# One plain pair of tiles instead of two at the start of three gated inputs, with the token scale moved between the products that follow

## The chip, the cores and the metric

The kernel runs on one core of one Trainium2 chip. The metric is the device time of one execution in microseconds. Three timed executions of the kernel before took 2118.08, 2118.48 and 2118.67 us, so the median is 2118.48 us. The profile comes from one further execution of the same program.

## The reference

A decoder trunk of two layers over 512 tokens with a model width of 1024, in float32. Each layer is a half-weighted gated network, a token mixer (retention in the first layer, attention with forget gates in the second), a second half-weighted gated network, and a gated input embedding; a root-mean-square norm stands ahead of each. What matters here is the gated network, of which there are four:

```python
def rmsnorm(x, w):
    xf = x.astype(jnp.float32)
    y = xf * lax.rsqrt(jnp.mean(xf * xf, axis=-1, keepdims=True) + EPS)
    return (y * w.astype(jnp.float32)).astype(x.dtype)

def swiglu(x, w_in, w_out):
    g, u = jnp.split(x @ w_in, 2, axis=-1)
    return (jax.nn.silu(g) * u) @ w_out
...
        h = h + 0.5 * swiglu(rmsnorm(h, nw[0]), ffn_w_in[i, 0], ffn_w_out[i, 0])
```

`w_in` is 1024 x 5632, that is 22 blocks of 128 gate columns and 22 blocks of 128 up columns.

## The kernel before

Every product is done with split numbers: a weight or an activation x is held as a high part (x rounded to the fast matmul type) and a low part (x minus the high part), and a product is three matmuls: high by high, high by low, low by high. The activations lie with the model width on the partitions and the 512 tokens along the free axis.

**A gated input** is the product of the normalised activations with one block of gate columns and one block of up columns, both 128 wide. There are 22 of these pairs for each of the four networks, which are called the first to fourth gated input here; in the code `i` is 0 to 3. Two loaded tiles of 128 x 1024 belong to each pair, `q` and `r`, and a pair is computed in one of two ways:

- *plain* (`plain` in `ffn`, matmuls on line 636): for each half of the tokens, eight blocks of the width, two outputs and three matmuls, so 96 matmuls of 128 x 256. Both tiles are split into high and low parts.
- *by seven* (class `Strassen`, matmuls on line 559 in `product`): the 2 x 2 block product with seven products in place of eight, each of 12 matmuls of 128 x 256, so 84 matmuls. `begin` does three of them: the first on `q` itself (`b11`), the second and third on two sums of the weights (`t1` on `s[0]`, `t2` on `s[1]`); it then adds partial results in PSUM (lines 584 to 588) and ends with `W.next_sums`, which lets the next pair's sums be built. `rest` does the other four, and `join` two more additions (lines 606 to 608).

The sums are built in `emit_sums_now`: four additions of weight quarters on the vector engine (line 168), each then split by a cast on the scalar engine (line 88) and a subtraction on the vector engine (line 89). One quarter (`x`, tile `a12`) and the `q` tile of most pairs get their low part in another way (`negated`, lines 134 to 136): two passes on the scalar engine, then a DMA from the GpSimd queue that adds the weights from HBM. Pairs marked `direct` split their `q` with lines 88 and 89. Raw weights come on the SP queue (line 80) into four buffers `wraw`; a later load waits until an earlier tile's readers are done with its buffer.

The **norm's token scale** is a number for each token. It isn't applied to the activations but to the products. `n.columns()` sums the squares over the partitions (eight small matmuls, line 367), and takes the inverse root: line 520 on the vector engine, the square root on the scalar engine (line 509, after a load of its table where another one is in), then lines 514 to 517 on the vector engine. `n.rows()` (line 504) turns the result by four matmuls into a row for each partition, which the scalar engine copies out of PSUM (line 498). `gated` then needs it: line 644 multiplies by it, line 645 takes the sigmoid-weighted unit, line 647 multiplies by the other half.

**Start of a gated input.** The list `PLAIN` says how many pairs begin plainly: `(3, 2, 2, 2)`. In the second to fourth gated input, plain pair 0 runs first; it takes the quarters of the activations block by block as the vector and scalar engines deliver them. Plain pair 1 then has the columns and the permission for the first sums at its step 3 (`summed`) and the rows at its step 10 (`scaled`) of 16. Then pairs 2, 3 and so on go by seven, each begun one pair ahead of its rest.

**Order.** Only the tensor engine's order is that of the program. The order on the vector, scalar and GpSimd engines and the queues is laid down by a scheduler when the program is built, from what can run when by its own costs; on the chip each engine then works through its list in that fixed order. PSUM has eight banks of 128 x 512, taken in rotation.

Of the kernel before, what the change touches and what calls it, by code (L numbers as in the profile page):

```python
# [29 lines left out]
KEPT = 7  # L30
STEP = 1024 + 48
WIDE = 2048 + 128
PLAIN = (3, 2, 2, 2)
CHUNKS = [((0, 6), (6, 14), (14, 22)) for n in PLAIN]
H2 = S // 2
HALVES = (slice(0, H2), slice(H2, S))
# [184 lines left out]
def trunk(ctx, tc, a):  # L221
# [16 lines left out]
    W = Weights(tc, wraw, wpool)  # L238

    def unit(pool):  # L240
        return pool.tile([P, S], F32R, name="unit_" + {id(ua): "a", id(ub): "b", id(uc): "c", id(ud): "d"}[id(pool)])
# [4 lines left out]
    for i in range(4):  # L246
        ins = [Pair(i, a["ffn_w_in"][i, m, 0], a["ffn_w_in"][i, m, 1]) for m in range(NF)]
        chunks = CHUNKS[i]
        outs = [[a["ffn_w_out"][i, m][:, k0 * P : k1 * P] for m in range(KB)] for k0, k1 in chunks]
        for m in [PLAIN[i]] + [k1 + 1 for _, k1 in chunks[:-1]]:  # L250
            ins[m].direct = ins[m + 1].direct = True
# [6 lines left out]
    for kind, hd in ret_order:  # L258
        i = at[kind] + (hd if kind in "qk" else 2 * (hd - 1))
# [10 lines left out]
    def plan_ffn(i):  # L270
        ins, outs = ffn_src[i]
        at = PLAIN[i]
        for pair in ins[:at]:
# [54 lines left out]
    def bank():  # L328
        return psum.tile([P, S], F32, name="bank")

    def temp(dtype=F32):
        return tmp.tile([P, S], dtype, name="tmp")
# [7 lines left out]
    def split(src, hi, lo, scale=None):  # L340

        if scale is None:
            high = nc.scalar.copy(hi, src)
            low = nc.vector.tensor_tensor(out=lo, in0=src, in1=hi.bitcast(F32), op=ALU.subtract)
        else:
            high = nc.scalar.activation(hi, src, AF.Identity, scale=scale)
            low = nc.vector.scalar_tensor_tensor(
                out=lo, in0=src, scalar=scale, in1=hi.bitcast(F32), op0=ALU.mult, op1=ALU.subtract
            )
        return high, low  # L350
# [205 lines left out]
    def product(out, w, c, forms, name, first=False):  # L556

        xs = [form[name] for form in forms]
        add = lambda w, x, start, stop: nc.tensor.matmul(  # L559
            out, w, x, start=start, stop=stop, skip_group_check=True  # L560
        )
        for j, (xh, xl) in enumerate(xs):
            wh = w[:, 0, c + j * P : c + (j + 1) * P]
            add(wh, xh, first and j == 0, False)
            add(wh, xl, False, False)
        for j, (xh, xl) in enumerate(xs):
            add(w[:, 1, c + j * P : c + (j + 1) * P], xh, False, j == 3)

    class Strassen:
# [2 lines left out]
        def __init__(self, n):  # L572
            self.n, self.live = n, {}

        def begin(self, pair):
            c0, c1 = HALVES
            forms = self.n.forms
            W.take(pair)
            g, u = bank(), bank()
            product(g[:, c0], pair.t[0], 0, forms, "b11", True)  # L580
            product(g[:, c1], pair.s[0], 0, forms, "t1")
            product(u[:, c1], pair.s[1], 0, forms, "t2", True)
            cc = temp()
            nc.scalar.copy(cc, g)
            nc.vector.tensor_tensor(out=u[:, c1], in0=u[:, c1], in1=cc[:, c0], op=ALU.add)
            u2 = temp()[:, c0]
            nc.scalar.copy(u2, u[:, c1])
            last = nc.vector.tensor_tensor(out=g[:, c1], in0=g[:, c1], in1=u2, op=ALU.add)
            self.live[id(pair)] = g, u, cc
            W.next_sums(last)  # L590
# [20 lines left out]
    def ffn(i, n, nxt, stack, apool, meanwhile=None):  # L611


        ins, outs = ffn_src[i]
        chunks = CHUNKS[i]
        c0, c1 = HALVES
        act, by7 = {}, Strassen(n)

        def plain(m, between={}):

            ws = [W.take(ins[m].q), W.take(ins[m].r)]
            g, u = bank(), bank()
            order = [(k, t) for k in range(KB) for t in range(2)]
            if i == 2:
                order.sort(key=lambda kt: (kt[0] >= KB - 2, kt[1]))
            elif i:
                order.sort(key=lambda kt: kt[1])
            for at, (k, t) in enumerate(order):
                if at in between:
                    between[at]()  # L630
                e = k % 2
                for o, (w, c) in ((g, (ws[e], 0)), (u, (ws[1 - e], 512))):
                    ks = slice(c + k // 2 * P, c + (k // 2 + 1) * P)
                    xh, xl = n.forms[k // 2][f"b{1 + e}{1 + t}"]
                    for q, (x, y) in enumerate(((w[0], xh), (w[0], xl), (w[1], xh))):
                        nc.tensor.matmul(  # L636
                            o[:, HALVES[t]], x[:, ks], y, start=k == t == q == 0, stop=k == KB - 1 and q == 2,
                            skip_group_check=True,
                        )
            return g, u  # L640

        def gated(m, g, u, change_sign):
            sg = temp()
            nc.vector.tensor_tensor(out=sg, in0=g, in1=n.r, op=ALU.mult)
            nc.scalar.activation(sg, sg, AF.Silu)
            if change_sign:
                nc.vector.scalar_tensor_tensor(out=sg, in0=u, scalar=-1.0, in1=sg, op0=ALU.mult, op1=ALU.mult)
            else:
                nc.vector.tensor_tensor(out=sg, in0=u, in1=sg, op=ALU.mult)
            hi, lo = unit(apool), unit(apool)  # L650
            split(sg, hi, lo)
            act[m] = hi, lo

        def out_blocks(c, ms):
            k0, k1 = chunks[c]
            os, ws = [bank() for _ in ms], [W.take(outs[c][m]) for m in ms]
            for k in range(k0, k1):
                js = slice((k - k0) * P, (k - k0 + 1) * P)
                for o, (wh, wl) in zip(os, ws):
                    mm3(o, wh[:, js], wl[:, js], *act[k], k == k0, k == k1 - 1)  # L660
            for m, o in zip(ms, os):
                if m == KB - 1 and c == len(chunks) - 1 and nxt.early and nxt.extra:
                    nxt.corner(range(KB // 2))
                t1 = temp()
                nc.vector.scalar_tensor_tensor(  # L665
                    out=t1, in0=o, scalar=-0.5, in1=n.r, op0=ALU.mult, op1=ALU.mult
                )
                nc.vector.tensor_tensor(out=h[m], in0=h[m], in1=t1, op=ALU.add)
                if c == len(chunks) - 1:
                    nxt.block(m)  # L670

        done = PLAIN[i]
        if i:
            whole = [plain(0)]
        else:
            W.look = LOOKAHEAD + 2
            W.place(ins[1])
            whole = [plain(0)]
            W.look = LOOKAHEAD
            whole.append(plain(1, {12: n.columns}))  # L680
            W.begin(())

        def scaled():
            n.rows()
            for m, (g, u) in enumerate(whole):
                gated(m, g, u, True)

        def summed():
            n.columns()
            W.begin((n.last,) if n.early else ())  # L690

        last = plain(done - 1, {3: summed, 10: scaled} if i else {10: scaled})
        by7.begin(ins[done])
        gated(done - 1, *last, True)
        begun = done + 1
        for c, (k0, k1) in enumerate(chunks):
            for m in range(done, k1):
                if begun < k1:
                    by7.begin(ins[begun])
                    begun += 1  # L700
                by7.rest(ins[m])
                gated(m, *by7.join(ins[m]), False)
            done = k1
            if begun < NF:
                by7.begin(ins[begun])
                begun += 1
            else:
                stack.close()
                if meanwhile:
                    meanwhile()  # L710
            pair = [(0, 1)] if done == NF else [(0,), (1,)]
            for ms in pair + [(m,) for m in range(2, KB)]:
                out_blocks(c, ms)
# [15 lines left out]
    class OutBoth:  # L729
# [5 lines left out]
        def add(self, i, m, ks_=range(4)):  # L735
            srcs, yhi, ylo = self.parts[i]
            if (i, m // 2) not in self.ws:
                self.ws[i, m // 2] = W.take(srcs[m // 2])
            wh, wl = self.ws[i, m // 2]
            for k in ks_:  # L740
                ks = slice((4 * (m % 2) + k) * P, (4 * (m % 2) + k + 1) * P)
                mm3(self.banks[m], wh[:, ks], wl[:, ks], yhi[k], ylo[k], i == 0 and k == 0, i == 1 and k == 3)
# [857 lines left out]
```

## Time and profile before

| | |
|---|---|
| median of three timed executions | 2118.48 us |
| the profiled execution's own time | 2118.82 us |
| its span from the first to the last instruction | 2117.0 us |
| mean granted clock of the tensor engine | 0.999 |
| tensor engine busy | 2102.4 us, 99% of the span |
| vector engine busy | 1573.0 us, 74% |
| scalar engine busy | 1276.7 us, 60% |
| GpSimd busy | 266.6 us, 13% |
| DMA | 299.46 MB, mean 141 GB/s |

The profiled execution is 0.34 us above the median. Between its own time and its span lie 1.8 us of start and end. In the rows of a timeline the first number is the start in microseconds from the span's start, the second the length of the row, then come engine, line, operation, output and input tiles, shapes and the count of merged instructions; a bracket names how long the engine was idle just before and what released it. Matmuls overlap, so the pace of a run of matmuls is read from start to start, not from their lengths. PE is the tensor engine, DVE the vector engine, ACT the scalar engine, POOL GpSimd.

### The profile page before, as it was taken

The page shows a single profiled execution, that of the slowest core. Times are in us where ns is not written, and L with a number is a line of the kernel's source. Part 1 is how long each engine was busy: PE and PEld are TensorE (multiplying, and loading weights), DVE is VectorE, ACT ScalarE, POOL GpSimd, SP SyncE. Part 2 cuts the span into 40 slices and gives each one's busy share as a digit, 9 for nine tenths or more (in the row PEclk, how much of TensorE's full clock was granted, in tenths as well). Part 3 has the DMA queues.
Part 4 walks back from the last instruction along what each step waited for, and adds up shares of the span by engine and source line. Part 5 has one row for each costly group of instructions (what it writes and reads, how often), then busy time and mean ns, then how long its engine had stood idle before and what let it go on. Part 6 is the DMA issues. An engine that isn't in the chain of part 4 may idle for free.

```text
span 2117.0 us, 36225 instructions
## 1 busy us (share of the span) xinstructions
PE 2102.4 (99%) x14155; PEld 1932.4 (91%) x14155; DVE 1573.0 (74%) x2915; ACT 1276.7 (60%) x2201; POOL 266.6 (13%) x282
## 2 busy tenths in 40 slices
PE   9999999999999999999999999999999999999998
PEld 9999998999998898989989999998888899999988
DVE  9786868677667886868768786776675687867775
ACT  8474556555665664737457465555796774645555
POOL 0010100121200010201001010110334200101100
PEclk9999999999999999999999999999999999999999
DMA  6575654666875354846435475563322335755631
GB/s 194 125 176 134 157 139 131 184 190 181 241 200 159 100 140 112 192 125 163 126 106 152 126 177 142 144 150 107 114 88 72 110 101 127 181 141 143 157 110 41
DMA packets 106285, 299.46 MB, mean 141 GB/s; under 512 B 11120, under 2 KB 14704, under 8 KB 106112
## 3 DMA queue, kind: packets, MB, share of 16 engines
q1 hardware_dynamic: 65088, 212.92, 30.8%
q0 software_dynamic: 36336, 76.82, 20.3%
q10 hardware_dynamic: 4688, 7.39, 1.0%
q8 instruction: 111, 1.82, 0.3%
q14 instruction: 62, 0.51, 0.1%
HBM read 284.47 MB, written 12.62 MB: 140 GB/s over the span
## 4 chain that ended last, share of the span: by engine, by line
PE 88%; DVE 4%; issue 4%; ACT 2%; DMA 1%; POOL 0%; SPq 0%; POOLq 0%; ACTq 0%; DVEq 0%
PE bank L559 41%; PE bank L354 12%; PE bank L353 12%; PE bank L355 12%; PE bank L636 4%; PE bank L544 1%; DMA w<-in_ret_p 1%; PE bank L843 1%; PE bank L844 1%; PE bank L845 1%; PE bank L777 1%; PE bank L778 1%; PE bank L779 1%; PE bank L1229 1%; DVE w L89 1%
## 5 line engine op out<-in xcount | busy, mean ns | idle before, releaser
L88 ACT CAST w<-wraw 128x1024 fp32r<-128x1024 f32 (+1 forms) x208 | 210.4, 1018 | 305.0 <-PE bank L355 210.2
L559 PE MATMUL bank<-unit_a,s 128*128 128x256 f32 x2202 | 322.5, 276 | 0.0
L88 ACT CAST s<-sums 128x512 fp32r<-128x512 f32 x372 | 219.9, 617 | 169.5 <-PE bank L559 82.6
L89 DVE TENSOR_TENSOR s<-sums,s 128x512 fp32r<-128x512 f32 x372 | 246.4, 686 | 101.6 <-ACT s L88 101.0
L559 PEld LDWEIGHTS bank<-unit_a,s 128*128 128x128 f32 x2202 | 284.7, 188 | 0.0
L353 PE MATMUL bank<-unit_d,w 128*128 128x512 f32 x656 | 255.7, 390 | 0.3 <-DVE tmp L1246 0.3
L354 PE MATMUL bank<-unit_d,w 128*128 128x512 f32 x656 | 255.3, 389 | 0.0
L355 PE MATMUL bank<-unit_d,w 128*128 128x512 f32 x656 | 255.3, 389 | 0.0
L89 DVE TENSOR_TENSOR w<-wraw,w 128x1024 fp32r<-128x1024 f32 (+1 forms) x186 | 218.3, 1174 | 44.4 <-ACT w L88 44.0
L559 PE MATMUL bank<-unit_b,s 128*128 128x256 f32 x1040 | 220.4, 276 | 0.0
L355 PE MATMUL bank<-unit_a,w 128*128 128x512 f32 (+1 forms) x536 | 198.3, 370 | 1.2 <-DVE w L89 1.2
L353 PE MATMUL bank<-unit_a,w 128*128 128x512 f32 (+1 forms) x536 | 199.4, 372 | 0.0
L354 PE MATMUL bank<-unit_a,w 128*128 128x512 f32 (+1 forms) x536 | 198.3, 370 | 0.1
L665 DVE SCALAR_TENSOR_TENSOR tmp<-bank,rows 128x512 f32<-128x512 f32 x96 | 66.1, 689 | 145.8 <-PE bank L355 145.8
L559 PEld LDWEIGHTS bank<-unit_b,s 128*128 128x128 f32 x1040 | 165.4, 188 | 0.0
L559 PE MATMUL bank<-unit_b,w 128*128 128x256 f32 x837 | 153.6, 281 | 0.5 <-DMA w<-in_ret_p 0.5
L136 POOL DMA_DIRECT2D a<-in_ffn_w_in x80 | 70.2, 877 | 651.2 <-ACT a L135 469.6
L559 PE MATMUL bank<-unit_a,w 128*128 128x256 f32 x978 | 149.6, 278 | 0.0
L559 PE MATMUL bank<-unit_c,s 128*128 128x256 f32 x682 | 149.2, 276 | 0.0
L353 PEld LDWEIGHTS bank<-unit_d,w 128*128 128x128 f32 x656 | 123.2, 188 | 25.8 <-DVE tmp L1246 0.5
L355 PEld LDWEIGHTS bank<-unit_d,w 128*128 128x128 f32 x656 | 123.1, 188 | 25.7
L354 PEld LDWEIGHTS bank<-unit_d,w 128*128 128x128 f32 x656 | 123.2, 188 | 25.1
(350 smaller groups left out, 4810.2 us busy)
## 6 DMA issues: line engine op xcount, KB each, us to landing
wraw<-in_ffn_w_in SPq DMA_DIRECT2D x174, 512.0 KB, 4.4
wraw<-in_ffn_w_out SPq DMA_DIRECT2D x64, 512.0 KB, 4.3
w<-in_ffn_w_in POOLq DMA_DIRECT2D x57, 512.0 KB, 5.6
a<-in_ffn_w_in POOLq DMA_DIRECT2D x79, 256.0 KB, 6.1
wraw<-in_ret_p SPq DMA_DIRECT2D x28, 512.0 KB, 3.6
wraw<-in_ffn_w_out SPq DMA_DIRECT2D x32, 384.0 KB, 3.6
kept<-tmp POOLq DMA_DIRECT2D x40, 256.0 KB, 4.0
wraw<-in_ret_v SPq DMA_DIRECT2D x16, 512.0 KB, 4.5
```

Of the source, the lines that this page charges most:

```text
L88: self.cast = self.nc.scalar.copy(hi, raw)
L89: low.tensor_tensor(out=lo, in0=raw, in1=hi.bitcast(F32), op=ALU.subtract)
L136: self.nc.gpsimd.dma_start(out=lo, in_=src, accum_op=ALU.add)
L353: nc.tensor.matmul(out, wh, xh, start=first, stop=False)
L354: nc.tensor.matmul(out, wh, xl, start=False, stop=False)
L355: nc.tensor.matmul(out, wl, xh, start=False, stop=last)
L544: nc.tensor.matmul(o[:, half], w[:, ks], x, start=k == t == q == 0, stop=k == KB - 1 and q == 2, skip_group_check=True,)
L559: add = lambda w, x, start, stop: nc.tensor.matmul(out, w, x, start=start, stop=stop, skip_group_check=True)
L636: nc.tensor.matmul(o[:, HALVES[t]], x[:, ks], y, start=k == t == q == 0, stop=k == KB - 1 and q == 2, skip_group_check=True,)
L665: nc.vector.scalar_tensor_tensor(out=t1, in0=o, scalar=-0.5, in1=n.r, op0=ALU.mult, op1=ALU.mult)
L777: nc.tensor.matmul(os[t], xh, wh[:, js], start=k == 0, stop=False)
L778: nc.tensor.matmul(os[t], xh, wl[:, js], start=False, stop=False)
```

## The change

`PLAIN` becomes `(3, 1, 1, 1)`, so pair 1 of the second to fourth gated input goes by seven instead of plainly. The permission for the first sums (`W.begin`) moves into plain pair 0, at its step 3. `begin` gets a function that it calls between its first and its second product: pair 1's `begin` has `n.columns` there, pair 2's `begin` has `scaled` (the rows and the gating of plain pair 0). Pair 1's rest follows without a new `begin` ahead of it, and from pair 2 on the order is as it was. The marks `direct` move with `PLAIN` to pairs 1 and 2 (before, 2 and 3). The first gated input stays as it is.

```diff
-PLAIN = (3, 2, 2, 2)
+PLAIN = (3, 1, 1, 1)
...
-        def begin(self, pair):
+        def begin(self, pair, between=None):
             c0, c1 = HALVES
             forms = self.n.forms
             W.take(pair)
             g, u = bank(), bank()
             product(g[:, c0], pair.t[0], 0, forms, "b11", True)
+            if between:
+                between()
             product(g[:, c1], pair.s[0], 0, forms, "t1")
             product(u[:, c1], pair.s[1], 0, forms, "t2", True)
...
         done = PLAIN[i]
+
+        def summed():
+            W.begin((n.last,) if n.early else ())
+
         if i:
-            whole = [plain(0)]
+            whole = [plain(0, {3: summed})]
...
-        def summed():
-            n.columns()
-            W.begin((n.last,) if n.early else ())
-
-        last = plain(done - 1, {3: summed, 10: scaled} if i else {10: scaled})
-        by7.begin(ins[done])
-        gated(done - 1, *last, True)
-        begun = done + 1
+        if i:
+            by7.begin(ins[done], n.columns)
+            by7.begin(ins[done + 1], scaled)
+            begun = done + 2
+        else:
+            last = plain(done - 1, {10: scaled})
+            by7.begin(ins[done])
+            gated(done - 1, *last, True)
+            begun = done + 1
         for c, (k0, k1) in enumerate(chunks):
             for m in range(done, k1):
-                if begun < k1:
+                if begun < min(k1, m + 2):
                     by7.begin(ins[begun])
                     begun += 1
                 by7.rest(ins[m])
```

The scheduler lays the other engines' lists anew around this. Two places in the fourth gated input show how; the numbers behind `s_` and `w_` tell buffers apart, and line numbers from 576 on are two higher in the changed kernel (584 to 588 read 586 to 590).

On the vector engine, from just ahead of the columns' first step (line 520) to the token scale itself (line 517, output `cols`), before:

```order
L168 TENSOR_TENSOR sums<-wraw 128x512
L520 TENSOR_SCALAR cv<-bank 128x4
L89 TENSOR_TENSOR s_19339<-sums,s_19339 128x512
L168 TENSOR_TENSOR sums<-sums,wraw 128x512
L89 TENSOR_TENSOR s_19363<-sums,s_19363 128x512
L168 TENSOR_TENSOR sums<-sums,wraw 128x512
L514 RECIPROCAL cols<-ct 128x4
L168 TENSOR_TENSOR sums<-wraw 128x512
L515 TENSOR_TENSOR ct<-cols 128x4
L89 TENSOR_TENSOR s_19366<-sums,s_19366 128x512
L516 SCALAR_TENSOR_TENSOR ct<-ct,cv 128x4
L517 SCALAR_TENSOR_TENSOR cols<-ct,cols 128x4
```

and in the changed kernel, where `s_19276` is the second sum of pair 2:

```order
L89 TENSOR_TENSOR s_19276<-sums,s_19276 128x512
L168 TENSOR_TENSOR sums<-wraw 128x512
L520 TENSOR_SCALAR cv<-bank 128x4
L587 TENSOR_TENSOR bank<-bank,tmp 128x256
L89 TENSOR_TENSOR s_19278<-sums,s_19278 128x512
L514 RECIPROCAL cols<-ct 128x4
L515 TENSOR_TENSOR ct<-cols 128x4
L590 TENSOR_TENSOR bank<-bank,tmp 128x256
L516 SCALAR_TENSOR_TENSOR ct<-ct,cv 128x4
L168 TENSOR_TENSOR sums<-wraw 128x512
L517 SCALAR_TENSOR_TENSOR cols<-ct,cols 128x4
```

Line 520 now stands behind all sums of pairs 1 and 2 but one split, and the two additions in PSUM that end pair 1's `begin` stand between line 520 and line 517, with a sum of pair 3's freshly loaded weights.

On the scalar engine at the same place, before:

```order
L88 CAST s_19340<-sums 128x512
L88 CAST s_19339<-sums 128x512
L88 CAST s_19363<-sums 128x512
L509 ACT_TABLE_LOAD
L509 ACTIVATE ct<-cv 128x4
L88 CAST s_19366<-sums 128x512
L498 COPY rows<-bank 128x512
```

and in the changed kernel:

```order
L88 CAST s_19276<-sums 128x512
L586 COPY tmp<-bank 128x512
L134 CAST w_19375<-wraw 128x2x512
L88 CAST s_19278<-sums 128x512
L135 ACTIVATE w_19375<-wraw 128x2x512
L509 ACT_TABLE_LOAD
L509 ACTIVATE ct<-cv 128x4
L589 COPY tmp<-bank 128x256
L88 CAST s_19447<-sums 128x512
L498 COPY rows<-bank 128x512
```

The root (line 509) now stands behind the cast of pair 2's second sum, the copy of pair 1's products (586) and both passes over pair 3's `q` (134 and 135, `w_19375`). The buffer of `s_19276` is that of pair 1's first sum, which pair 1's second product reads. In the second gated input the two lists are much the same (the cast of `s_19278` stands ahead of 134 there), without the table load; in the third the copy of pair 1's products (586) stands three casts earlier, and pair 2's `x` (134) ahead of pair 1's first sum.

## The prediction

> **What bounds the kernel now.** First the page's busy times, then the tensor engine's list of waits, then its timeline at the start of each of the three gated inputs that change. The fourth stands for them here, with the fourth pair's products and some of the second and third.
>
> ```profile
> PE 2102.4 (99%) x14155; PEld 1932.4 (91%) x14155; DVE 1573.0 (74%) x2915; ACT 1276.7 (60%) x2201; POOL 266.6 (13%) x282
> ...
> PE bank L504 <- DVE rn L517: 0.9, 1, 0.9
> ...
> 746.92 2.31 PE L636 MATMUL bank<-unit_b,w 128*128 128x256 f32 x18
> ...
> 1138.61 2.31 PE L636 MATMUL bank<-unit_b,w 128*128 128x256 f32 x18
> ...
> 1719.20 2.31 PE L636 MATMUL bank<-unit_b,w 128*128 128x256 f32 x18
> ...
> 1721.35 0.95 PE L367 MATMUL bank<-ones_r,tmp 128*128 128x2 f32 x8
> 1722.16 0.96 PE L636 MATMUL bank<-unit_c,w 128*128 128x256 f32 x6
> ...
> 1727.28 0.60 PE L504 MATMUL bank<-ident,cols 128*128 128x128 f32 x4
> 1727.63 0.96 PE L636 MATMUL bank<-unit_d,w 128*128 128x256 f32 x6
> ...
> 1732.02 0.64 PE L559 MATMUL bank<-unit_b,w 128*128 128x256 f32 x4
> ...
> 1736.18 0.64 PE L559 MATMUL bank<-unit_b,w 128*128 128x256 f32 x4
> ...
> 1740.34 0.39 PE L559 MATMUL bank<-unit_b,w 128*128 128x256 f32 x2
> ...
> 1745.78 0.64 PE L559 MATMUL bank<-unit_b,w 128*128 128x256 f32 x4
> ```
>
> The tensor engine is the bound: busy 99%, and whatever it no longer does is time saved, as long as nothing makes it wait. Its rows also show the one wait of this kind that exists: the transposes (504) once waited 0.9 us for line 517, elsewhere in the program. In the three starts nothing waits there: the columns (367) end at 1722.16, the rows begin at 1727.28, 5.12 us of plain matmuls lie between.
>
> **What is removed and added on the tensor engine.** Plain pair 1 runs from 1719.20 to 1732.02, 12.82 us. Less the columns (1721.35 to 1722.16, 0.81) and the rows (1727.28 to 1727.63, 0.35), which stay, its 96 matmuls take 11.66. By seven, a `begin` takes 4.16 (1732.02 to 1736.18) and a `rest` 5.44 (1740.34 to 1745.78), together 9.60. Each gated input saves 2.06 us, the three 6.2 us.
>
> **What moves closer together.** The columns now stand behind pair 1's first product, the rows behind pair 2's first. A product on `w` has 12 matmuls at 0.12 (18 take 1721.35 - 1719.20 = 2.15), so 1.44; the other two of a `begin` share 4.16 - 1.44, so 1.36 each. From the end of plain pair 0, at t0, the tensor engine would end the columns at t0 + 2.25, pair 1's second product at t0 + 3.61, its third at t0 + 4.97, and wants the scale (517) at t0 + 6.41. Between columns and rows lie 4.16 us in place of 5.12, and the lists of the two other engines have changed more than that. These rows price them:
>
> ```profile
> 1717.00 0.69 DVE L168 TENSOR_TENSOR sums<-wraw 128x512 f32<-128x512 f32 x1
> ...
> 1718.38 0.69 DVE L89 TENSOR_TENSOR s<-sums,s 128x512 fp32r<-128x512 f32 x1
> ...
> 1722.34 0.16 DVE L520 TENSOR_SCALAR cv<-bank 128x4 f32<-128x4 f32 x1 [0.26 <-PE bank L367]
> ...
> 1722.75 1.28 ACT L509 ACT_TABLE_LOAD   x1
> ...
> 1724.04 0.21 ACT L509 ACTIVATE ct<-cv 128x4 f32<-128x4 f32 x1
> ...
> 1726.45 0.16 DVE L517 SCALAR_TENSOR_TENSOR cols<-ct,cols 128x4 f32<-128x4 f32 x1
> ...
> 1733.33 1.05 ACT L134 CAST w<-wraw 128x1024 fp32r<-128x1024 f32 x1
> 1734.28 1.05 ACT L135 ACTIVATE w<-wraw 128x1024 fp32r<-128x1024 f32 x1
> 1735.24 0.60 ACT L88 CAST s<-sums 128x512 fp32r<-128x512 f32 x1
> 1735.75 0.57 ACT L584 COPY tmp<-bank 128x512 f32<-128x512 f32 x1
> 1736.94 0.37 ACT L587 COPY tmp<-bank 128x256 f32<-128x256 f32 x1 [0.62 <-DVE bank L585]
> ...
> 1737.42 0.42 DVE L588 TENSOR_TENSOR bank<-bank,tmp 128x256 f32<-128x256 f32 x1
> ...
> wraw<-in_ffn_w_in SPq DMA_DIRECT2D x174, 512.0 KB, 4.4
> ```
>
> Before, line 520 ran 0.2 us after the columns and 517 was done at 1726.61, 0.7 us ahead of need. Now the scalar engine's root (509) stands behind the cast of pair 2's second sum, and that cast needs the buffer that pair 1's *second product* reads. So the scale can't begin its way before that product has left the array: t0 + 3.61, and the last matmul's 0.17 us of tail. From there, in the fourth gated input (t0 = 1719.20, product gone at 1722.98): cast 0.60, copy 0.5 (1735.24 and 1735.75 are that far apart) to 1724.1. Pair 3's raw weights are there by about then: their buffer is free when pair 1's third sum has been formed, some 0.5 us after t0, and the load takes 4.4. Passes 134 and 135 over them take 0.95 and 1.05 with a cast of 0.55 between: 1726.7. The table takes 1.28, the root 0.21: 1728.2. Then 0.2 to line 514, the copy and addition that end pair 1's `begin` (0.37 and 0.42), 515, 516 and 517 at 0.16 each and a sum of 0.69 between the last two, 1.85 us with their handovers: **the scale at 1730.1, wanted at 1725.6, a wait of 4.5 us**. Behind the waiting transposes stand all matmuls that follow, so the wait counts in full.
>
> The second gated input (t0 = 746.92) needs no table: product gone at 750.7, cast, copy, cast, 134, 135 and root to 754.6, the scale at 756.4, wanted at 753.3: **3.0 us**. The third needs these rows:
>
> ```profile
> 1136.91 0.68 DVE L168 TENSOR_TENSOR sums<-wraw 128x512 f32<-128x512 f32 x1
> ...
> 1138.46 0.62 ACT L134 CAST a<-wraw 128x512 fp32r<-128x512 f32 x1 [0.20 <-PE bank L636]
> ```
>
> There the cast of pair 1's first sum stands behind pair 2's `x` (134), which waits for plain pair 0 to leave its buffer until 1138.46; so pair 1's third sum is formed only at about 1142.1, pair 3's load lands at 1146.6, and two passes, a cast, table and root bring it to 1150.7, the scale to 1152.5. Wanted at 1138.61 + 6.41 = 1145.0: **7.5 us**. Bounds: with the load already landed, the scalar engine's list alone gives 5.5 in the third; with every load 1 us later 8.5, and 5.5 in the fourth. Together 15.0, between 13 and 17.5.
>
> **What the waits do to the clock.** No wait of several microseconds stands inside the trace of before; its two ends are the nearest rows.
>
> ```profile
> 1.59 4.21 PE L338 MATMUL bank<-tmp,ones_r 128*128 128x512 f32 x9 [1.59 <-DVE tmp L336]
> ...
> 5.60 1.41 PE L636 MATMUL bank<-unit_b,w 128*128 128x256 f32 x6
> ...
> 6.84 0.88 PE L636 MATMUL bank<-unit_d,w 128*128 128x256 f32 x6
> ...
> 2105.30 2.33 PE L1413 MATMUL bank<-unit_a,ones_r 128*128 128x512 f32 x9
> ...
> 2107.46 0.56 PE L1422 MATMUL bank<-ones_r,tmp 128*128 128x2 f32 x4
> ...
> 2110.23 0.59 PE L1443 MATMUL bank<-tmp,ones_r 128*128 128x256 f32 x2
> ...
> 2111.00:2112.00 1.00, 0.00 (x0) 0.00 (x0) 1.00 (x4) 0.23 (x1) 0.69 (x2) 1.00 0.26 92
> 2112.00:2113.00 1.00, 0.00 (x0) 0.00 (x0) 0.51 (x2) 0.00 (x0) 0.72 (x2) 0.64 0.63 216
> ```
>
> In the stretches, the number behind POOL is the granted clock. The last matmul ends at 2110.82; 0.64 over the next-to-following microsecond means full clock until 2112.28 and half from then: 1.5 us after the last matmul, with gaps before it. At the start nine matmuls of 128 x 512 take 4.01 us (1.59 to 5.60) against 2.16 for the same nine at full clock (2105.30 to 2107.46), and the next six lose 0.53 (1.41 against 0.88): a cold start loses 2.4 us. A wait costs between nothing (clock held) and 2.4 more. The waits of 4.5 and 7.5 us are three and five times what sufficed at the end, so I take 2.4 for each, and half, 1.2, for that of 3.0, which a busy stretch precedes: 6.0 in all.
>
> [...]
>
> [...]
>
> **What costs nothing.** Each of the three gets one pair more of sums, additions and, for the second and fourth, two DMAs from the GpSimd queue.
>
> ```profile
> 759.74:773.50 13.76, 13.76 (x122) 13.76 (x121) 10.36 (x18) 11.17 (x18) 2.16 (x2) 1.00 0.49 116
> ```
>
> In a stretch of pairs by seven the vector engine is busy 10.36 of 13.76 us, the scalar engine 11.17, the DMA engines half: matmuls cover it, as they do for the twenty other pairs. Uncovered, eight operations of 0.69 would be 5.5 us for each. Pair 1's first two sums are wanted 2.25 and 3.61 us behind t0; in the fourth gated input the vector engine is done with the quarters at about 1716 and needs four steps of 0.65, so they are there by 1719.2, in time. In the third, pair 1's `q` is now split on the vector engine (1.22) in place of a DMA, in a stretch that has about that much room; at worst 1 us, inside the bounds.
>
> **The sum**, against the profiled execution's 2118.82: less 6.2, plus 15.0 of waits, plus 6.0 of clock is 2133.6, +0.70%. The median of the runs lies 0.34 lower, so **2133.3 us**.
>
> **Rivals.**
>
> 1. *The clock holds.* [...] For it: 0.999 over the whole span, in spite of waits of up to 0.9. Against it: the 1.5 us at the end. 2118.5 - 6.2 + 15.0 = 2127.3 (2125 to 2130 by the bounds).
> 2. *The scale is in time, and the saving stands* (the other side): 2118.5 - 6.2 = 2112.3. It takes the root to be free of the casts ahead of it. For it: before, a like list gave it within 4.45 us of the columns (1722.16 to 1726.61), against 4.16 now. Against it: the engines' lists are fixed, and each holds a wait for pair 1's second product ahead of the root. It would turn from slower to faster where the three waits sum to under 6.2, some 2 us each: in the second gated input about 1 us of the scalar engine's work between that product and the root would have to fall away, in the fourth 2.5, in the third 5.5.
> 3. *Waits about as long as the saving*, 4 to 8 us in all with the clock held: 2116 to 2121, no change that can be told. It needs the load and half the scalar work to overlap in a way the lists don't show.
> 4. *More is late*: the loads that pile up behind the waits and the colder clock make later pairs wait as well, each 2 us more: over 2139. Against it: pair 3's `begin`, the next to want sums, comes over 8 us behind the rows.
>
> **How the numbers follow.** The forecast (2128 to 2139, late scale and halved clock) has 0.50, the clock that holds 0.22, the saving that stands 0.10, waits about equal to it 0.08, more late work 0.10. Differences under 0.2% (4.2 us) I count as no change, about what a measurement of this kernel tells. Faster is then 0.10, same 0.08, slower 0.82. For the range: from the late scale with the clock held and a short chain, some way into rival 3, up to where rival 4 begins: 2120 to 2139, which leaves out 0.10 of rival 2, most of rival 4 and a little of rival 3.
>
> **What would show it.** In the timeline of the changed kernel, three idle stretches of the tensor engine ahead of line 504, released by line 517, of about 3, 7.5 and 4.5 us; line 509 starting behind line 135; 36 matmuls fewer on the tensor engine; and matmuls behind each wait at nearly twice their pace, with a granted clock under 1. If line 504 starts 6.4 us behind plain pair 0 in all three, the reasoning on the lists is wrong; if the waits are there and the clock stays at 1.00, only its term is.

## The result, and the profile after

| | before | changed |
|---|---|---|
| median of four timed executions | 2118.57 us | 2132.57 us (2131.78 to 2136.69) |
| ratio, with its 95% interval | | 1.0071 (1.0059 to 1.0083) |
| span of the profiled execution | 2117.0 us | 2130.0 us |
| mean granted clock | 0.999 | 0.996 |
| matmuls | 14155 | 14119 |

The change makes the kernel 14.0 us slower; the forecast was 2133.3 us, 14.8 slower. The changed kernel's list of waits on the tensor engine (what waits, what it waits for, us in total, times, longest) has a new first line:

```profile
PE bank L504 <- DVE cols L517: 13.6, 3, 7.3
PE bank L338 <- DVE tmp L336: 1.6, 1, 1.6
```

Three waits, one in each changed gated input. These are rows of the changed kernel's timeline on the tensor engine. For the second gated input they show the first product of pair 1's `begin`, the columns, the first product of pair 2's `begin`, the transposes with the idle time ahead of them, and the first matmul of pair 3's `begin`; for the third and fourth only the first, the fourth and the last of these (pair 2's `begin` starts at 1146.60 and 1734.36 there).

```profile
747.00 0.64 PE L559 MATMUL bank<-unit_b,w 128*128 128x256 f32 x4
...
748.43 0.95 PE L367 MATMUL bank<-ones_r,tmp 128*128 128x2 f32 x8
...
752.16 0.65 PE L559 MATMUL bank<-unit_b,w 128*128 128x256 f32 x4
...
756.14 0.65 PE L504 MATMUL bank<-ident,cols 128*128 128x128 f32 x4 [2.38 <-DVE cols L517]
...
766.65 0.64 PE L559 MATMUL bank<-unit_b,w 128*128 128x256 f32 x4
...
1141.44 0.65 PE L559 MATMUL bank<-unit_b,w 128*128 128x256 f32 x4
...
1155.48 1.11 PE L504 MATMUL bank<-ident,cols 128*128 128x128 f32 x4 [7.29 <-DVE cols L517]
...
1166.26 0.64 PE L559 MATMUL bank<-unit_b,w 128*128 128x256 f32 x4
...
1729.21 0.64 PE L559 MATMUL bank<-unit_b,w 128*128 128x256 f32 x4
...
1739.90 1.12 PE L504 MATMUL bank<-ident,cols 128*128 128x128 f32 x4 [3.94 <-DVE cols L517]
...
1750.34 0.64 PE L559 MATMUL bank<-unit_b,w 128*128 128x256 f32 x4
```

From the end of plain pair 0 to pair 3's `begin` the kernel before needs 12.82 + 4.16 = 16.98 us (plain pair 1 and pair 2's `begin`). The changed kernel needs 766.65 - 747.00 = 19.65 us in the second gated input and 1166.26 - 1141.44 = 24.82 in the third. In the fourth it is 1750.34 - 1729.21 = 21.13. That is 2.67, 7.84 and 4.15 us more, 14.7 together; the other 2000 us differ by -1.7 in the two profiled executions (their spans by 13.0), 1.2 of it a wait of line 355 for line 89 late in the kernel before that the changed kernel's list does not show.

The scalar engine of the changed kernel in the fourth gated input shows why the scale is late:

```profile
1733.19 0.62 ACT L88 CAST s<-sums 128x512 fp32r<-128x512 f32 x1 [1.07 <-PE bank L559]
1733.84 0.59 ACT L586 COPY tmp<-bank 128x512 f32<-128x512 f32 x1
1734.32 1.05 ACT L134 CAST w<-wraw 128x1024 fp32r<-128x1024 f32 x1
1735.27 0.62 ACT L88 CAST s<-sums 128x512 fp32r<-128x512 f32 x1
1735.79 1.06 ACT L135 ACTIVATE w<-wraw 128x1024 fp32r<-128x1024 f32 x1
1736.86 1.28 ACT L509 ACT_TABLE_LOAD   x1
1738.15 0.21 ACT L509 ACTIVATE ct<-cv 128x4 f32<-128x4 f32 x1
```

The first cast waits for the tensor engine, that is for pair 1's second product to be done with the buffer; then the copy, the two passes, another cast, the table and the root follow without a gap. On the vector engine of the same stretch the columns' first step was done three microseconds before the root, and what comes after the root takes 1.5 us:

```profile
1735.06 0.15 DVE L520 TENSOR_SCALAR cv<-bank 128x4 f32<-128x4 f32 x1
...
1738.39 0.18 DVE L514 RECIPROCAL cols<-ct 128x4 f32<-128x4 f32 x1 [1.78 <-ACT ct L509]
1738.61 0.16 DVE L515 TENSOR_TENSOR ct<-cols 128x4 f32<-128x4 f32 x1
1738.68 0.43 DVE L590 TENSOR_TENSOR bank<-bank,tmp 128x256 f32<-128x256 f32 x1
1739.02 0.15 DVE L516 SCALAR_TENSOR_TENSOR ct<-ct,cv 128x4 f32<-128x4 f32 x1
1739.09 0.69 DVE L168 TENSOR_TENSOR sums<-wraw 128x512 f32<-128x512 f32 x1
1739.69 0.16 DVE L517 SCALAR_TENSOR_TENSOR cols<-ct,cols 128x4 f32<-128x4 f32 x1
```

The busy times of the changed kernel by stretches hold the second loss. Each stretch is 3.41 us long; the columns are length, busy us (and instructions) of the tensor engine, of its weight load, of the vector, scalar and GpSimd engines, then the granted clock, the DMA engines' share and GB/s:

```profile
753.27:756.69 3.42, 1.04 (x10) 0.82 (x9) 2.69 (x10) 2.16 (x5) 1.07 (x1) 1.00 0.74 250
756.69:760.10 3.41, 3.41 (x18) 3.41 (x18) 2.56 (x6) 1.30 (x4) 0.00 (x0) 0.50 1.10 228
760.10:763.51 3.41, 3.41 (x31) 3.41 (x31) 1.80 (x3) 3.25 (x4) 0.00 (x0) 1.00 0.42 147
...
1152.63:1156.05 3.42, 0.57 (x3) 0.57 (x4) 2.04 (x7) 2.15 (x4) 1.07 (x1) 0.50 1.02 302
1156.05:1159.46 3.41, 3.41 (x18) 3.41 (x17) 2.68 (x6) 2.71 (x5) 0.00 (x0) 0.50 0.65 116
...
1739.73:1743.14 3.41, 3.24 (x15) 3.24 (x16) 3.27 (x7) 2.56 (x4) 0.00 (x0) 0.50 0.88 164
```

Behind each wait the clock is 0.50: 18 matmuls fit where 31 fit a stretch later. The engine counts as busy all the while: its busy time is 2103.2 us, 0.8 more than before, although 36 matmuls are gone. Where this time went is read from the clock column.

### The profile page after: what moved, and what is told of

Its sections match the earlier page's. It is cut to its first block, busy times and chain, and to the rows that moved or that the text cites. A ratio compares the mean times of both kernels' runs of the same rounds, so it can differ in the third digit from the quotient of the medians.

```text
span 2130.0 us, 36208 instructions
## 1 busy us (share of the span) xinstructions
PE 2103.2 (99%) x14119; PEld 1933.3 (91%) x14119; DVE 1586.7 (74%) x2947; ACT 1288.9 (61%) x2226; POOL 270.7 (13%) x286
## 4 chain that ended last, share of the span: by engine, by line
PE 90%; DVE 5%; ACT 3%; issue 1%; DMA 1%; POOL 0%; SPq 0%; POOLq 0%; ACTq 0%; DVEq 0%
PE bank L559 43%; PE bank L354 12%; PE bank L353 12%; PE bank L355 12%; PE bank L638 2%; PE bank L851 1%; PE bank L852 1%; PE bank L850 1%; PE bank L544 1%; DMA wraw<-in_ffn_w_in 1%; PE bank L784 1%; PE bank L786 1%; PE bank L785 1%; PE bank L1236 1%; PE bank L1250 0%
## 5 line engine op out<-in xcount | busy, mean ns | idle before, releaser
L88 ACT CAST s<-sums 128x512 fp32r<-128x512 f32 x384 | 227.5, 618 | 185.6 <-PE bank L559 94.8
L559 PE MATMUL bank<-unit_a,s 128*128 128x256 f32 x2259 | 333.4, 277 | 0.0
L89 DVE TENSOR_TENSOR s<-sums,s 128x512 fp32r<-128x512 f32 x384 | 254.3, 686 | 105.8 <-ACT s L88 104.8
L559 PEld LDWEIGHTS bank<-unit_a,s 128*128 128x128 f32 x2259 | 294.4, 189 | 0.0
L89 DVE TENSOR_TENSOR w<-wraw,w 128x1024 fp32r<-128x1024 f32 (+1 forms) x182 | 213.2, 1172 | 39.2 <-ACT w L88 38.8
L559 PE MATMUL bank<-unit_b,s 128*128 128x256 f32 x1076 | 231.1, 279 | 0.0
L559 PEld LDWEIGHTS bank<-unit_b,s 128*128 128x128 f32 x1076 | 172.7, 190 | 0.1
L559 PE MATMUL bank<-unit_b,w 128*128 128x256 f32 x864 | 158.8, 282 | 0.0
L559 PE MATMUL bank<-unit_c,s 128*128 128x256 f32 x706 | 155.7, 278 | 0.0
L559 PE MATMUL bank<-unit_a,w 128*128 128x256 f32 x1005 | 154.1, 278 | 0.0
```

The source lines that it names most:

```text
L88: self.cast = self.nc.scalar.copy(hi, raw)
L89: low.tensor_tensor(out=lo, in0=raw, in1=hi.bitcast(F32), op=ALU.subtract)
L559: add = lambda w, x, start, stop: nc.tensor.matmul(out, w, x, start=start, stop=stop, skip_group_check=True)
```

## The experiments

Each kernel is timed against the kernel before on the same chip. Beside the filled waits, the rows later, the root first and both edits together the kernel before took 2118.29 us; beside the two halves and the third left as it was, it took 2117.60. "Added" is the time from plain pair 0's end to pair 3's `begin` less the 16.98 us of the kernel before, in the second, third and fourth gated input; the changed kernel adds 2.67, 7.84 and 4.15.

**Is the loss behind the waits one of the clock?** Matmuls of no use fill the waits; the transposes then overwrite their bank.

```diff
     def spread(c, fill=()):
         o = bank()
+        for x in fill:
+            nc.tensor.matmul(o[:, 0:H2], ones_r, x, start=True, stop=True, ...)
...
-            n.rows()
+            n.rows((0, 21, 62, 34)[i])
```

> The changed kernel with matmuls of no use put ahead of the transposes (line 504): 21, 62 and 34 of 128 x 256 at about 0.118 us, that is 2.5, 7.3 and 4.0 us, close to the three gaps of 2.55, 7.44 and 4.10 us in its trace. Nothing else moves. My theory (late scale, and a clock that halves because the tensor engine is idle): the scale comes as late as before, but the clock stays at 1.00, and about 5.0 us come back, 2127.5 us. If the 5 us behind the waits come from something else that the wait brings (late sums, late weights, banks), the time stays at 2132.6. If the clock falls for lack of useful progress on other engines, the same.

Measured: 2128.49 us, ratio 1.0045 (1.0031 to 1.0059). The scale is no earlier, so this kernel waits as long as the changed one, only busily. In its timeline:

```profile
753.53 2.54 PE L505 MATMUL bank<-unit_b,ones_r 128*128 128x256 f32 x21
756.09 0.65 PE L507 MATMUL bank<-ident,cols 128*128 128x128 f32 x4
...
1153.95 0.65 PE L507 MATMUL bank<-ident,cols 128*128 128x128 f32 x4 [0.30 <-DVE cols L520]
```

(its lines from 504 on are three higher.) Its clock stays 1.00 in all three stretches behind the transposes:

```profile
756.00:760.00 4.00, 3.98 (x36) 3.91 (x36) 3.96 (x8) 3.00 (x5) 0.00 (x0) 1.00 1.07 257
1153.00:1160.00 7.00, 6.70 (x58) 6.50 (x57) 5.67 (x12) 5.07 (x8) 0.00 (x0) 1.00 0.72 156
1736.00:1743.00 7.00, 7.00 (x62) 6.85 (x62) 5.58 (x12) 5.22 (x8) 0.00 (x0) 1.00 0.82 193
```

Added: 0.83, 6.08 and 2.38, together 5.4 us less than in the changed kernel. The time is 4.1 us lower by the medians and 5.5 by the two ratios. So some 5 us were lost to the clock, because the engine stood idle, and not to work that came late behind the waits.

**Is it the late scale?** The rows and the gating of plain pair 0 are wanted later, behind the first product of pair 1's `rest`, and nothing else is changed.

```diff
-            by7.begin(ins[done + 1], scaled)
+            by7.begin(ins[done + 1])
...
-                by7.rest(ins[m])
+                by7.rest(ins[m], scaled if i and m == 1 else None)
```

> The changed kernel with the rows and the gating of plain pair 0 moved from between the first two products of pair 2's begin to behind the first product of pair 1's rest, 4.4 us later for the tensor engine; the lists of the vector and scalar engines up to the token scale are row for row those of the changed kernel. Theory (nothing but the late scale costs): the scale is there 9.05, 13.95 and 10.6 us behind plain pair 0 and is wanted at 10.9, so only the third gated input still waits, 3.0 us, with some 1.7 us of clock: 2118.6 - 4.4 + 3.0 + 1.7 = 2118.9 us, between 2116 and 2121. Rival (the first two products of a begin, late sums or weights cost it, not the scale): the waits stay where they are and the time stays at 2130 or more. Rival (the wait only moves on): pair 3's begin waits for the banks of plain pair 0, which are then free about 4 us behind the rows: some 2 us each in the second and fourth, 2122 to 2125.

Measured: 2119.56 us, ratio 1.0007 (0.9998 to 1.0016); no wait for line 517 is left in the three starts. Added: -1.47, 3.89 and 0.16. The second gated input has its saving, undisturbed. The other two still wait, but for something else:

```profile
1151.64 0.79 PE L559 MATMUL bank<-unit_b,w 128*128 128x256 f32 x2 [3.79 <-ACT tmp L589]
...
1733.02 0.50 PE L559 MATMUL bank<-unit_b,w 128*128 128x256 f32 x2 [1.36 <-ACT tmp L589]
```

Pair 1's rest waits for the copy that ends pair 1's `begin` (589, 587 before). On the scalar engine that copy stands right behind the root. So moving the rows takes away the wait for the scale, and what stands next behind the same root is wanted just ahead of the rows' new place. Neither my theory nor the rival on banks had that. The total came out as expected, the places only in part: the third waits 3.8 us in place of 3.0, the fourth 1.4 in place of none. In the fourth the root itself is later than in the changed kernel, done 10.6 us behind plain pair 0 in place of 9.2: in this profile the first pass over pair 3's weights waits 1.36 us for their load, which it did not there. So this short wait hangs on the load as well as on the order.

**What in the lists makes it late?** Here the rows stay where the change put them, and only the lists are altered: pair 3's passes are queued behind the root, and its sums behind line 517. `n.columns()` returns these two instructions, the root and line 517; `W.look` is one lower for the first `begin`, so that pair 3 is taken up by pair 2's.

```diff
+            scale = []
+            W.look = LOOKAHEAD - 1
-            by7.begin(ins[done], n.columns)
-            by7.begin(ins[done + 1], scaled)
+            by7.begin(ins[done], lambda: scale.extend(n.columns()))
+            W.look = LOOKAHEAD
+            by7.begin(ins[done + 1], scaled, scale)
...
-            W.take(pair)
+            with ExitStack() as order:
+                for ins in behind:
+                    order.enter_context(tc.issue_after(ins.ins))
+                W.take(pair)
```

> The changed kernel with only the lists changed: pair 3's two passes (134, 135) stand behind the root (509) on the scalar engine, and pair 3's sums behind line 517 on the vector engine. My theory says that these, with their 2.0 us and 0.7 us and the wait for pair 3's load, are part of the chain to the scale: the three waits fall from 2.55, 7.44, 4.10 to about 0.9, 5.5 and 2.4 us, the clock is kept in the second gated input, and the time is 2125.7 us (2123 to 2128). Rival (the vector engine's sums for pair 2 alone set line 520 and with it the scale; what stands ahead of the root only fills time): the waits stay within 0.5 us of what they are, 2131 to 2133.

Measured: 2122.56 us, ratio 1.0022 (1.0013 to 1.0031). The rows in its timeline:

```profile
754.58 0.65 PE L504 MATMUL bank<-ident,cols 128*128 128x128 f32 x4 [0.94 <-DVE cols L517]
...
1149.61 1.11 PE L504 MATMUL bank<-ident,cols 128*128 128x128 f32 x4 [4.29 <-DVE cols L517]
...
1732.38 0.65 PE L504 MATMUL bank<-ident,cols 128*128 128x128 f32 x4 [1.56 <-DVE cols L517]
```

Waits of 6.8 us in all in place of 13.6, and only behind the longest of them do the four transposes take 1.11 us in place of 0.65, as they do at half clock. What this run moves, pair 3's passes and sums, is thus half of the lateness. I had expected less of it (8.8 us of waits left, and 2123 to 2128).

The other half is left, and the rows of this run say where it lies. Line 520 still stands behind all sums of pairs 1 and 2 on the vector engine and is done at 753.48, 1148.09 and 1730.85; the root follows within 0.3 us each time, in the second gated input after a wait for it:

```profile
753.52 0.20 ACT L509 ACTIVATE ct<-cv 128x4 f32<-128x4 f32 x1 [1.03 <-DVE cv L520]
```

In the third and fourth the table is loaded at about the same moment (to 1148.16 and 1731.09). So what the rival named, the vector engine's sums ahead of line 520, is the next queue in line, alone in the second gated input and beside the table's load in the others. No run here moves it.

The same with each half alone, first the scalar engine's passes (`scale.extend(n.columns()[:1])`):

> As the run with the root first, but on the vector engine pair 3's sums are left where the scheduler puts them, ahead of line 517; only the scalar engine's two passes (134, 135) stand behind the root (509). Theory (the scalar engine's passes and the load they wait for were the larger part of the chain): the waits stay near those of the run with both edits (1.1, 4.5, 1.7 us), plus up to 1.4 us where two sums of 0.69 stand between lines 520 and 517; the sums also wait for pair 3's second tile, which may bring back more in the third: 1.5 to 2, 5 to 6.5, 2 to 3 us, 2124 to 2128 us. Rival (the sums on the vector engine alone held the scale): the waits go back to 2.5, 7.4 and 4.1.

and then the vector engine's sums (`scale.extend(n.columns()[1:])`):

> The other half: pair 3's sums stand behind line 517, and the two passes stand ahead of the root again, as in the changed kernel (in the fourth gated input one of the two). Theory: the waits shrink by no more than the one sum of 0.69 us, to 1.9, 6.8 us, and to 2.4 in the fourth, where one pass of 1.0 us is gone as well; 2129 to 2131 us. Rival (the sums held the scale): the waits fall to 1.1, 4.5 and 1.7 us as with both edits, 2122.6.

Measured: 2129.98 us, ratio 1.0058 (1.0040 to 1.0076), and 2129.64 us, ratio 1.0056 (1.0038 to 1.0075). The waits are 2.16, 7.42 and 3.15 us with the passes alone moved, and 1.91, 7.82 and 2.51 with the sums alone. So in the third gated input neither half helps. For the sums alone the time came as expected, and so did the waits but for the third (7.82 us in place of 6.8). My expectation that the scalar engine's passes were the larger part is wrong (2129.98 us in place of 2124 to 2128): with them behind the root, this stood on the vector engine of that kernel instead, in the third gated input:

```profile
1152.11 0.69 DVE L168 TENSOR_TENSOR sums<-wraw 128x512 f32<-128x512 f32 x1 [1.42 <-DMA wraw<-in_ffn_w_in]
1152.84 0.69 DVE L168 TENSOR_TENSOR sums<-sums,wraw 128x512 f32<-128x512 f32 x1
1153.45 0.17 DVE L514 RECIPROCAL cols<-ct 128x4 f32<-128x4 f32 x1
```

Its root, on the scalar engine, was done at 1150.65, and the first of pair 3's passes followed:

```profile
1150.44 0.21 ACT L509 ACTIVATE ct<-cv 128x4 f32<-128x4 f32 x1
...
1150.99 1.05 ACT L134 CAST w<-wraw 128x1024 fp32r<-128x1024 f32 x1
```

Line 514 ran 2.8 us later, behind two sums of which the first had waited for a load of pair 3. It is the second of that pair's two tiles: the passes read the first, `q`, and ran without waiting for it, before the sums could. With the sums alone moved, the passes wait for the first tile on the scalar engine, ahead of the root:

```profile
1150.19 1.04 ACT L134 CAST w<-wraw 128x1024 fp32r<-128x1024 f32 x1 [2.32 <-DMA wraw<-in_ffn_w_in]
...
1152.73 1.28 ACT L509 ACT_TABLE_LOAD   x1
```

The two loads for pair 3 held the scale there by two roads of about one length (waits of 7.42 and 7.82 us for the scale), one through each engine. The rival that one engine alone sets it is wrong too; both roads must be cleared.

**Both edits together**, the root first and the rows later (the diffs are those above, with no function given to pair 2's `begin`):

> Both edits together. The scale comes some 7.5, 12.1 and 9.0 us behind plain pair 0, the rows are wanted at 10.9: only the third gated input waits, 1.2 us, too little for the clock. With the saving as the changed kernel's trace has it (1.5 us for each gated input, since the matmuls of pair 1 run at 0.118 us there) 2118.6 - 4.4 + 1.2 = 2115.4 us; with the saving as I predicted it (2.06 each) 2113.6. If pair 3's begin then waits for banks, sums or weights, 2117 to 2121.

Measured: 2115.73 us, ratio 0.9988 (0.9979 to 0.9997). Added: -1.48, -0.45 and -1.48; the third has a wait of 0.74 us for the copy, and pair 3's weights, now taken up later, cost 0.56 a little further on; 500 matmuls behind, the third is 1.37 us behind the kernel before. The two waits are 1.3 of the 2.85 us between this and the saving of the other two; the rest was not followed up.

**The third left as it was**, with columns and rows inside its plain pair 1 as before, and the rest as in the run above:

```diff
-PLAIN = (3, 1, 1, 1)
+PLAIN = (3, 1, 2, 1)
...
         def summed():
+            if done == 2:
+                n.columns()
             W.begin((n.last,) if n.early else ())
...
-            whole = [plain(0, {3: summed})]
+            whole = [plain(0, {3: summed} if done == 1 else {})]
...
-        if i:
+        if done == 1:
...
-            last = plain(done - 1, {10: scaled})
+            last = plain(done - 1, {3: summed, 10: scaled} if i else {10: scaled})
...
-                by7.rest(ins[m], scaled if i and m == 1 else None)
+                by7.rest(ins[m], scaled if PLAIN[i] == m == 1 else None)
```

> As the run with the root first and the rows later, but the third gated input keeps its two plain pairs, columns and rows included, as before. In that run the second and fourth gained 1.48 us each, and the third lost 1.37 through two short waits (the copy 589 behind the root, pair 3's weights). By regions, 2118.3 - 3.0 = 2115.3 us, a little under the 2115.7 of that run or up to 1.4 us lower, since its other 1 us came from elsewhere: 2114 to 2116. If the third's short waits were only moved from later, no difference from that run.

Measured: 2114.17 us, ratio 0.9984 (0.9975 to 0.9993). This is within what was expected, 3.4 us faster than the kernel before and the lowest time of these kernels; but its interval overlaps with that of the run above, so the two can't be told apart. Both gains are smaller than the 4.2 us that the prediction counts as no change, though their intervals lie below 1.

## Why the prediction was right, and where it was not

**The scale's time** was the step on which most rested, and it held. From plain pair 0's end, line 517 was forecast to be done after 9.5, 13.9 and 10.9 us and was done after 9.1, 14.0 and 10.6 (756.09, 1155.42 and 1739.85 in the changed kernel). The links were there as named: the cast that waits for pair 1's second product (in the second and fourth), the copy, both passes, in the third gated input a wait for pair 3's load (1.19 us), the table where one is loaded, the root, and a sum ahead of 517. What the prediction did not see is that the two engines' lists hold the scale separately: the halved experiments show that taking the passes away alone would have changed little.

**The waits**: forecast 3.0, 7.5 and 4.5 us, 15.0 in all. Reckoned as in the forecast, from where the transposes would have begun, they are 2.55 (756.14 less 752.16 + 1.43, the length of that product), 7.44 and 4.10: 14.1. The scale was wanted 6.6 us behind plain pair 0 instead of the 6.41 forecast, which shortens each wait by 0.2.

**The clock** was forecast to cost 2.4, 2.4 and 1.2 us, 6.0 in all, out of the cold start. With the 15.51 us that the second gated input takes when it neither waits nor falls (748.06 to 763.57 with the rows later), what is left of the measured stretches is 19.65 - 15.51 - 2.55 = 1.6, then 1.9 and 1.5: 5.0, and 5.4 by the filled waits. That the clock halves was right (0.50 behind all three waits), and the rival that it holds (2127.3) was not. The sizes were off both ways: each wait cost about the same, the short one too. By the stretches shown above, matmuls ran at half clock for 3.4, 4.0 and 3.2 us; half of that is lost, 1.7, 2.0 and 1.6. The cold start was no measure of it.

**The saving** was the term that was mis-sized most: forecast 2.06 us for each gated input, 6.2 in all; measured 1.47 or 1.48, 4.4 in all, in every place without a wait (rows later: second; both edits: second and fourth). The price of a `begin` and a `rest` was taken from the steady stretch behind the start (4.16 and 5.44 us). Pair 1's products take 1.43 and 2.91 in its `begin` and 5.65 in its `rest`, and pair 2's `begin` 4.34, because the matmuls run there at 0.118 us each, as the plain ones did, and not yet at the 0.113 of the steady stretch. Why they change pace only with pair 3's `begin` stays open.

**What costs nothing**: nothing more was late in the changed kernel, so the rival with more late work (over 2139) was not needed.

**The sum**: -4.4 + 14.1 + 5.0 = +14.7 in the three places against a forecast of -6.2 + 15.0 + 6.0 = +14.8. The terms were off by +1.8, -0.9 and -1.0, which nearly cancel: that the total was so close is luck.

**The rival of the other side**, a saving that stands (2112.3), was said to be on the faster side once the waits sum to less than the saving. The lists decide that as the prediction argued: with 6.8 us of waits the kernel is still slower (2122.56), with under 2 it is faster (2115.73, 2114.17).

## What to carry to other kernels

A value that a saturated engine needs soon is as late as the longest queue in front of any of its steps: before its consumer is moved closer, look on every engine of its chain for what stands ahead in the fixed list and what that in turn waits for, loads above all. When one road is cleared, see which one ends next; here two roads led through the loads of one pair, and only when both were cleared and the consumer was moved back as well did 14 us lost turn into some 3 gained. Price a moved piece of work from rows at the place where it will run, and count for a wait on the tensor engine not only its length but also the slow stretch that can follow, which counts as busy (here 1.7, 2.0 and 1.6 us lost).

## What was not expected of the hardware

**The clock behind the waits.** In the changed kernel the granted clock is 0.50 in three places inside the program: from 756.69 to 760.10 us, from 1152.63 to 1159.46 and from 1739.73 to 1743.14, that is for 3.41, 6.83 and 3.41 us. The tensor engine had gone idle 2.93, 4.44 and 3.77 us before these falls, so not one fixed time ahead. At the last matmuls, the kernel before fell to half clock after a stretch of 3.41 us with 1.56 us busy, and the kernel with the rows later kept full clock after one with 1.73 us busy:

```profile
2108.86:2112.27 3.41, 1.56 (x6) 0.68 (x4) 2.55 (x9) 0.37 (x1) 0.96 (x2) 1.00 0.11 38
2112.27:2115.68 3.41, 0.00 (x0) 0.00 (x0) 0.24 (x1) 0.00 (x0) 0.45 (x1) 0.50 0.77 269
```

```profile
2110.27:2113.68 3.41, 1.73 (x7) 0.84 (x5) 2.44 (x10) 0.37 (x1) 0.80 (x2) 1.00 0.10 36
2113.68:2117.09 3.41, 0.00 (x0) 0.00 (x0) 0.40 (x2) 0.00 (x0) 0.61 (x1) 1.00 0.79 272
```

Waits of about 2 us went both ways in the second gated input. With the sums alone moved, the engine waited 1.91 us, from 755.12 to 757.03, and the clock stayed at 1.00; with the passes alone moved it waited 2.16 us, from 753.51 to 755.67, and the clock fell to 0.50 at 755.52:

```profile
753.00:756.42 3.42, 2.12 (x18) 1.91 (x16) 2.69 (x8) 3.23 (x6) 0.25 (x1) 1.00 0.69 149
756.42:759.83 3.41, 2.80 (x24) 2.80 (x25) 3.07 (x8) 2.09 (x3) 0.82 (x1) 1.00 1.03 332
```

```profile
752.10:755.52 3.42, 1.40 (x12) 1.20 (x11) 3.42 (x11) 2.39 (x5) 0.00 (x0) 1.00 0.73 184
755.52:758.93 3.41, 3.26 (x16) 3.27 (x17) 2.68 (x6) 2.84 (x5) 1.07 (x1) 0.50 0.84 217
```

No run here shows what decides between the two, and one profile of each kernel can't show how often such a wait costs the clock.

**Two paces of the same matmul.** At a granted clock of 1.00, matmuls of 128 x 256 follow each other every 0.113 us in the steady pairs by seven, and every 0.118 to 0.120 in most plain pairs, in the first product of every `begin`, and in the first pairs of a changed start. The same instructions ran at either pace in different kernels: 65 matmuls of a plain pair in the first gated input, with no wait among them, took 7.36 us in the kernel before (20.57 to 27.93) and 7.66 in the changed one (20.87 to 28.53). No experiment here tells why.
